# The mLSTM gates' running maximum: products by TensorE, or copies through DRAM by GpSimd

## The chip, the cores and the metric

The kernel is one program on one core of a Trainium2 chip. The metric is the time of one execution on the device, in microseconds (us), as the median of several runs; all inputs lie in the chip's memory beforehand. The difference treated here is a few microseconds of about two milliseconds.

## The reference

A trunk of four residual layers works on 256 tokens of width 2048: an even layer (sliding-window attention beside an mLSTM, one joint input projection), a SwiGLU layer, an odd layer (forgetting attention), another SwiGLU layer. Everything is float32. The change touches the mLSTM of the even layer alone: four heads, keys of width 128, values of width 256, two chunks of 128 tokens. What it computes of the gates:

```python
i_pre = softcap(i_m + b_i)                  # 256 x 4
f_pre = softcap(f_m + b_f)
log_f = jax.nn.log_sigmoid(f_pre)           # in chunks of 128
b = jnp.cumsum(log_f, axis=-1)
...
log_D = b[..., :, None] - b[..., None, :] + log_i[..., None, :]
log_D = jnp.where(causal, log_D, -jnp.inf)
g = b + m_prev[..., None]
m_t = jnp.maximum(g, jnp.max(log_D, axis=-1))
D = jnp.exp(log_D - m_t[..., None])
inter = jnp.exp(g - m_t)
qk = jnp.einsum('bhctd,bhcsd->bhcts', qc, kc) * D
```

The stabiliser m_t is a running maximum along the tokens, one for each head. It is needed in two layouts: along the free dimension, the same on all 128 partitions (for D, whose rows are keys and whose columns are queries), and with tokens on the partitions (for `inter` and the weights of the keys).

## The kernel before

**Matmuls.** Each float32 weight is split into a high and a low part in the reduced format fp32r, and each activation likewise, so that one product is three matmuls (high by high, low by high, high by low). Weights come from DRAM in chunks of 2 x 128 rows by 512 columns (512 KB) through the SyncE queue (L119); ScalarE casts the high part (L173, or L318 for derived operands), VectorE subtracts to get the low part (L174, L319), and TensorE multiplies: 512 columns a matmul. `gemm` walks the 16 tiles of k in eight steps of two. `pair_group` computes two projections at once with seven products in place of eight, over eight positions in an order written out by hand (`MIXQ`, `MIXV`); it derives sums and differences of the weight chunks on VectorE (tiles `hr`) and keeps its sums in PSUM banks of the pools `pa` and `pm`, four banks each.

**Side jobs.** Work that isn't a large matmul is put in between. A list `later` holds pairs of step and function, and `run_due` calls those that are due when a gemm gets to that step; `pair_group` has such a list of its own (`todo`). `Q_STEPS`, `OM_STEPS` and `VM_STEPS` say at which step of which projection each job comes:

- G0 to G4: the mLSTM's gates (below)
- S0 to S2: sums of activations for the seven-product form
- R0 to R3: the second halves of the four groups of sliding-window attention (products of the turned weights `tt` with the values `vs` into `po`, L449, split into `mh` and `ml`)
- J0: the end of one group's transposition by DMA

The projection of `OFF_OM` (o gate, 256 columns), then `OFF_VM` (values), then `pair_even` over the mLSTM's queries and keys (`OFF_QM`, `OFF_KM`) is the stretch from about 126 to 170 us of the profile. Inside it also run the last groups' soft-max (den, rec, `s` times `rec`, L391 and L395) and its transposes (L435, L439).

**Order.** The program is written with tile pools under a scheduler that plans with a timeline of its own and fixes the order of the instructions of each engine; semaphores hold the engines to the dependences. On each engine the order is strict: an instruction that waits holds up all behind it.

**The gates.** `gates_0` caps them and makes -log_sigmoid (`nlf`). `gates_1` makes, in PSUM, the input gate plus the sum of forget gates, with heads on four partitions (`ut`), then by two scans on VectorE the running maximum `mt` (4 x 256), with the chunk's last value in `edge` (4 x 2). `gates_2` fills a PSUM tile `pn` by ten small products: the sums of forget gates with tokens on partitions (`upper` by `nlf`, L880), `mt` turned (by the identity, K = 4, L881), and `edge` on all partitions (by the identity). VectorE copies it to `nat` and makes `un` and `ex`, and ScalarE takes the exponential of `ex`. `gates_3`, twice, for two heads each: four products in all of a selector `sel` (4 x 128, built by GpSimd) with `mt` put the rows of the maximum on all partitions (tile `pb`, L902), VectorE adds the mask `future` into `dt_` (L905), and ScalarE takes four exponentials with `un` as bias (L913). `dt_` is used after the query and key projection, `ex` in the scaling of queries and keys.

The odd layer uses another way for a quantity of the same kind: its summed forget gates are written to DRAM (`scratch`, L1119) and broadcast back to all partitions by GpSimd's queue (L1124), and GpSimd masks them (L1129).

Of the kernel before, what the change touches and what calls it, by code (L numbers as in the profile page):

```python
# [7 lines left out]
F32 = mybir.dt.float32  # L8
# [4 lines left out]
ALU = mybir.AluOpType  # L13
# [4 lines left out]
P = 128  # L18
D = 2048
S = 256  # L20
NT = S // P
KT = D // P
FF = 5632
NB = 512
CK = 2
EPS = 1e-5
NEG = -1.0e30
# [28 lines left out]
Q_STEPS = dict(S0=2, S1=4, R1=6, S2=6, G0=7)  # L56
OM_STEPS = dict(G1=1, J0=3, G2=4, R0=6, G3=7)
VM_STEPS = dict(R2=1, G4=1, R3=4)
PARTS = (0, 3, 7, 11)
# [9 lines left out]
def trunk(  # L69
# [651 lines left out]
    with tc.tile_pool(name="ev", bufs=1) as ev:  # L721
        with tc.issue_after(loaded[0].ins):
# [17 lines left out]
        )  # L740
        future = ev.tile([P, P], F32, name="future")
        nc.gpsimd.memset(future, 0.0)
        nc.gpsimd.affine_select(
            out=future, in_=future, pattern=[[1, P]], compare_op=ALU.is_ge, fill=-NEG, base=0, channel_multiplier=-1
        )

        nk = KVH * HD
# [99 lines left out]
        edge = ev.tile([4, 2], F32, name="edge")  # L847
        nat = ev.tile([P, 3, NT, 4], F32, name="nat")
        un = ev.tile([P, NT, 4], F32, name="un")
        ex = ev.tile([P, 4, 4], F32, name="ex")  # L850
        sel = ev.tile([4, ML_H, P], F32, name="sel")
        dt_ = None
# [7 lines left out]
        def gates_1():  # L860
            pu = pm.tile([P, NB], F32, tag="pm", name="pu")
            for c in range(NT):
# [11 lines left out]
                out=mt[:, P : 2 * P], data0=ut[:, P : 2 * P], data1=ut[:, P : 2 * P], initial=edge[:, 1:2], op0=ALU.max, op1=ALU.max  # L874
            )

        def gates_2():
            pn = pm.tile([P, NB], F32, tag="pm", name="pn")
            for c in range(NT):
                nc.tensor.matmul(pn[:, 4 * c : 4 * c + 4], upper, nlf[:, c, :], start=True, stop=True)  # L880
                nc.tensor.matmul(pn[:, 8 + 4 * c : 12 + 4 * c], mt[:, c * P : (c + 1) * P], ident[0:4, 0:4], start=True, stop=True)  # L881
                nc.tensor.matmul(
                    pn[:, 16 + 4 * c : 20 + 4 * c], edge[:, c : c + 1].broadcast_to([4, P]), ident[0:4, 0:4], start=True, stop=True
                )
            nc.vector.tensor_copy(nat.rearrange("p a c h -> p (a c h)"), pn[:, 0:24])
            nc.vector.tensor_tensor(out=un, in0=ig, in1=nat[:, 0, :, :], op=ALU.add)
            nc.vector.tensor_tensor(out=ex[:, 0:2, :], in0=nat[:, 0, :, :], in1=nat[:, 1, :, :], op=ALU.subtract)
            nc.vector.tensor_tensor(out=ex[:, 2, :], in0=nat[:, 2, 1, :], in1=nat[:, 1, 1, :], op=ALU.subtract)
            nc.vector.tensor_tensor(out=ex[:, 3, :], in0=un[:, 0, :], in1=nat[:, 2, 0, :], op=ALU.subtract)
            nc.scalar.activation(ex, ex, AF.Exp)  # L890

        def gates_3(g):
            nonlocal dt_
            if g == 0:
                dt_ = ev.tile([P, ML_H, NT, P], F32, tag="dt", name="dt_")
                nc.gpsimd.memset(sel, 1.0)
                nc.gpsimd.affine_select(
                    out=sel, in_=sel, pattern=[[-1, ML_H], [0, P]], compare_op=ALU.is_equal, fill=0.0, base=0, channel_multiplier=1
                )
            pb = pm.tile([P, 2, NT, P], F32, tag="pm", name="pb")  # L900
            for i in range(2):
                nc.tensor.matmul(  # L902
                    pb[:, i, :, :].rearrange("p c q -> p (c q)"), sel[:, 2 * g + i, :], mt, start=True, stop=True
                )
            nc.vector.tensor_tensor(  # L905
                out=dt_[:, 2 * g : 2 * g + 2, :, :].rearrange("p h c q -> p (h c) q"),
                in0=pb.rearrange("p h c q -> p (h c) q"),
                in1=future[:, None, :].broadcast_to([P, 4, P]),
                op=ALU.add,
            )  # L910
            for hh in (2 * g, 2 * g + 1):
                for c in range(NT):
                    nc.scalar.activation(  # L913
                        dt_[:, hh, c, :], dt_[:, hh, c, :], AF.Exp, bias=un[:, c, hh : hh + 1], scale=-1.0
                    )
# [7 lines left out]

        jobs = dict(G0=gates_0, G1=gates_1, G2=gates_2, G3=lambda: gates_3(0), G4=lambda: gates_3(1))
        jobs.update((f"S{j}", lambda j=j: sums_q(j)) for j in range(len(mixed_of(MIXQ))))
# [31 lines left out]
        with tc.tile_pool(name="mp", bufs=1) as mp:  # L957
# [9 lines left out]

            def pair_even(c0, c1, order):
                plain, c = pair_group(mp, 0, x_of, sums_m, [(wi, c0), (wi, c1)], order, halves=halves, raws=raws, inner=lambda: None)
# [347 lines left out]
```

## Time and profile before

| | |
|---|---|
| median of 3 runs | 2084.02 us (2083.39 to 2084.61) |
| profiled execution, its own time | 2085.2 us |
| span of the profile | 2083.5 us |
| TensorE (PE) busy | 2073.6 us, 100% |
| VectorE (DVE) busy | 1826.7 us, 88% |
| ScalarE (ACT) busy | 1362.8 us, 65% |
| GpSimd (POOL) busy | 37.8 us, 2% |
| mean granted TensorE clock | 0.998 of full speed |
| DMA | 208 GB/s on average |

The profile is one execution, recorded by the hardware's profiler. Busy time is the union of the recorded instructions of an engine; a matmul's record overlaps with that of the next, so that the distance of their starts, not the length, is what one costs in a row. PEld is the loading of weights, beside PE. The granted clock is that at which TensorE was allowed to run, as a share of full speed. The chain of waits is followed back from the last instruction to whatever released it. Rows in order of time have the start, the length, the engine, the line of the program (L...), the operation, output and inputs, the shape, and how many of them follow one another; brackets hold a wait and what ended it. Rows by windows give, for each stretch of time, the sum and then the busy time and count of PE, PEld, DVE, ACT and POOL, then the granted clock, the share of time in which the DMA engines are busy, and what they move in GB/s.

### The profile page before, as it was taken

To read this page: it belongs to the slowest core of one execution; us is meant where nothing else is said; L and a number is where in the kernel's file an instruction comes from. 1 tells how busy PE (TensorE), PEld (TensorE's weight loads), DVE (VectorE), ACT (ScalarE), POOL (GpSimd) and SP (SyncE) were. 2 spreads that over 40 slices of the span, in tenths; PEclk is the share of its full clock that TensorE was granted. 3 is DMA by queue.
4 is the path that set the end of the run, shared out by engine and by line. 5 is a ranking of instruction groups with operands and counts; after the bars stand their busy time and mean duration, and the time that the engine had idled before them with its cause. 6 is when DMAs were issued, how large, how long until landed. Compare 5 with 4: busy or idle time off the path is not lost.

```text
span 2083.5 us, 27000 instructions
## 1 busy us (share of the span) xinstructions
PE 2073.6 (100%) x9513; PEld 1721.3 (83%) x9513; DVE 1826.7 (88%) x2416; ACT 1362.8 (65%) x1720; POOL 37.8 (2%) x62
## 2 busy tenths in 40 slices
PE   9999999999999999999999999999999999999998
PEld 7878888888888888888888888888888888888887
DVE  6778859999999999999898778679999999999994
ACT  6765568665576656667677777587655667456753
POOL 1000000000000000000000000000000000000000
PEclk9999999999999999999999999999999999999999
DMA  8664668666666666666666866586656667666664
GB/s 293 174 198 149 216 175 253 219 207 206 197 227 218 208 217 209 216 203 212 190 202 211 240 185 191 157 277 220 215 196 208 205 204 238 202 205 208 222 197 139
DMA packets 302616, 432.77 MB, mean 208 GB/s; under 512 B 99584, under 2 KB 107792, under 8 KB 302352
## 3 DMA queue, kind: packets, MB, share of 16 engines
q1 hardware_dynamic: 300432, 424.70, 64.3%
q0 software_dynamic: 1328, 5.26, 0.7%
q8 instruction: 75, 1.23, 0.2%
q10 hardware_dynamic: 720, 1.09, 0.2%
q14 instruction: 61, 0.50, 0.1%
HBM read 408.15 MB, written 2.11 MB: 197 GB/s over the span
## 4 chain that ended last, share of the span: by engine, by line
PE 97%; DVE 1%; ACT 1%; issue 0%; DMA 0%; SPq 0%; POOLq 0%; POOL 0%; ACTq 0%; DVEq 0%
PE acc L488 21%; PE acc L489 21%; PE acc L490 21%; PE acc L209 6%; PE acc L208 5%; PE acc L210 5%; PE prod L488 5%; PE prod L489 5%; PE prod L490 5%; PE p L348 1%; PE po L449 1%; ACT s L382 0%; PE ptm L338 0%; PE po L450 0%; DMA raw<-in_w_in_even_dram 0%
## 5 line engine op out<-in xcount | busy, mean ns | idle before, releaser
L173 ACT CAST hi<-raw 128x1024 fp32r<-128x1024 f32 (+3 forms) x656 | 665.3, 1028 | 445.5 <-PE acc L490 280.1
L174 DVE TENSOR_TENSOR lo<-raw,hi 128x1024 fp32r<-128x1024 f32 (+3 forms) x656 | 772.6, 1192 | 147.0 <-ACT hi L173 144.5
L489 PE MATMUL acc<-lo,xh 128*128 128x512 f32 x1254 | 489.7, 391 | 0.0
L488 PE MATMUL acc<-hi,xh 128*128 128x512 f32 x1254 | 486.3, 390 | 0.0
L490 PE MATMUL acc<-hi,xl 128*128 128x512 f32 x1254 | 485.6, 390 | 0.0
L490 PEld LDWEIGHTS acc<-hi,xl 128*128 128x128 f32 x1254 | 235.8, 188 | 49.1 <-issue 0.3
L488 PEld LDWEIGHTS acc<-hi,xh 128*128 128x128 f32 x1254 | 235.5, 188 | 49.1 <-ACT hi L173 0.2
L489 PEld LDWEIGHTS acc<-lo,xh 128*128 128x128 f32 x1254 | 235.9, 188 | 48.7 <-DVE lo L174 0.2
L489 PE MATMUL acc<-lo,mh 128*128 128x512 f32 x437 | 169.7, 389 | 0.0
L490 PE MATMUL acc<-hi,ml 128*128 128x512 f32 x437 | 168.2, 389 | 0.0
L488 PE MATMUL acc<-hi,mh 128*128 128x512 f32 x437 | 167.9, 389 | 0.0
L318 ACT CAST hi<-raw 128x512 fp32r<-128x512 f32 x109 | 67.7, 621 | 90.4 <-PE acc L490 82.7
L209 PE MATMUL acc<-lo,mh 128*128 128x512 f32 (+1 forms) x322 | 126.2, 392 | 0.0
L208 PE MATMUL acc<-hi,mh 128*128 128x512 f32 (+1 forms) x322 | 125.6, 391 | 0.1
L318 ACT CAST ht<-t 128x1024 fp32r<-128x1024 f32 x95 | 99.9, 1052 | 35.4 <-PE prod L490 33.0
L210 PE MATMUL acc<-hi,ml 128*128 128x512 f32 (+1 forms) x322 | 122.4, 390 | 0.0
L319 DVE TENSOR_TENSOR lt<-t,ht 128x1024 fp32r<-128x1024 f32 x95 | 115.7, 1218 | 4.2 <-ACT ht L318 4.2
L318 ACT CAST ht<-raw 128x1024 fp32r<-128x1024 f32 x95 | 99.7, 1049 | 28.5 <-PE acc L490 13.4
L319 DVE TENSOR_TENSOR lt<-raw,ht 128x1024 fp32r<-128x1024 f32 x95 | 115.7, 1218 | 1.4 <-ACT ht L318 1.3
L209 PE MATMUL acc<-lo,xh 128*128 128x512 f32 (+3 forms) x288 | 99.5, 347 | 0.2 <-DVE lo L174 0.2
L210 PE MATMUL acc<-hi,xl 128*128 128x512 f32 (+3 forms) x288 | 98.1, 344 | 0.0
L208 PE MATMUL acc<-hi,xh 128*128 128x512 f32 (+3 forms) x288 | 95.9, 347 | 0.3 <-ACT hi L173 0.2
(362 smaller groups left out, 3444.4 us busy)
## 6 DMA issues: line engine op xcount, KB each, us to landing
raw<-in_w_gate_dram SPq DMA_DIRECT2D x176, 512.0 KB, 4.4
raw<-in_w_up_dram SPq DMA_DIRECT2D x176, 512.0 KB, 4.6
raw<-in_w_down_dram SPq DMA_DIRECT2D x176, 512.0 KB, 5.1
raw<-in_w_in_odd_dram SPq DMA_DIRECT2D x88, 512.0 KB, 5.1
raw<-in_w_in_even_dram SPq DMA_DIRECT2D x51, 512.0 KB, 4.8
raw<-in_w_out_even_dram SPq DMA_DIRECT2D x32, 512.0 KB, 4.7
raw<-in_w_out_odd_dram SPq DMA_DIRECT2D x32, 512.0 KB, 4.6
hr<-in_w_in_even_dram SPq DMA_DIRECT2D x12, 512.0 KB, 4.6
```

The lines of the kernel that those rows point to most:

```text
L173: latest[0] = nc.scalar.copy(hi[:, k, 0:n], raw[:, k, 0:n])
L174: nc.vector.tensor_tensor(out=lo[:, k, 0:n], in0=raw[:, k, 0:n], in1=hi[:, k, 0:n].bitcast(F32), op=ALU.subtract)
L208: nc.tensor.matmul(o, ah[:, ts], hi, start=(k == 0), stop=False)
L209: nc.tensor.matmul(o, ah[:, ts], lo, start=False, stop=False)
L210: nc.tensor.matmul(o, al[:, ts], hi, start=False, stop=(k == k_all - 1 and cs.stop == n))
L318: nc.scalar.copy(dst_h, src)
L319: nc.vector.tensor_tensor(out=dst_l, in0=src, in1=dst_h.bitcast(F32), op=ALU.subtract)
L348: nc.tensor.matmul(pq[j % 2][:, j // 2, :], q_of(j, b), k_of(j)[:, 0:cols], start=True, stop=True)
L449: nc.tensor.matmul(po, v_of(j, 0), tt[:, j, 0:2, :].rearrange("p c q -> p (c q)"), start=True, stop=False)
L488: nc.tensor.matmul(o, ah, hi, start=start, stop=False)
L489: nc.tensor.matmul(o, ah, lo, start=False, stop=False)
L490: nc.tensor.matmul(o, al, hi, start=False, stop=stop)
```

## The change

The transposed maximum, its copies on all partitions and the edges no longer go over TensorE. `gates_1` also makes the two sums of forget gates (`upper` by `nlf`) into its own PSUM tile, copies them to `nat`, and writes `mt` and `edge` to two DRAM tiles, `rows` and `ends`, through GpSimd's queue. A new job GB (`gates_b`, step 4 of the o projection) reads them back through the same queue: `rows` on all partitions into `dt_` (512 KB), `ends` on all partitions into `edge_b`, and the two halves of `rows` turned into `nat` (one word for each token and head); two selects on GpSimd mask `dt_` (in place of the tile `future` and two additions on VectorE). `gates_2` keeps the small subtractions and one exponential and goes to step 5. The eight exponentials of `gates_3` go together into the query and key projection, at its position 4. R0 and R3 keep their steps; G3 and G4 are gone.

```diff
 Q_STEPS = dict(S0=2, S1=4, R1=6, S2=6, G0=7)
-OM_STEPS = dict(G1=1, J0=3, G2=4, R0=6, G3=7)
-VM_STEPS = dict(R2=1, G4=1, R3=4)
+OM_STEPS = dict(G1=1, J0=3, GB=4, G2=5, R0=6)
+VM_STEPS = dict(R2=1, R3=4)
+G3_AT = 4
...
-        future = ev.tile([P, P], F32, name="future")
-        nc.gpsimd.memset(future, 0.0)
-        nc.gpsimd.affine_select(
-            out=future, in_=future, pattern=[[1, P]], compare_op=ALU.is_ge, fill=-NEG, base=0, channel_multiplier=-1
-        )
...
-        nat = ev.tile([P, 3, NT, 4], F32, name="nat")
+        nat = ev.tile([P, 2, NT, 4], F32, name="nat")
...
-        sel = ev.tile([4, ML_H, P], F32, name="sel")
+        rows = dp.tile([ML_H, S], F32, name="rows")
+        ends = dp.tile([ML_H, 2], F32, name="ends")
+        edge_b = ev.tile([P, ML_H, 2], F32, name="edge_b")
...
         def gates_1():
...
+            for c in range(NT):
+                nc.tensor.matmul(pu[:, 2 * P + 4 + 4 * c : 2 * P + 8 + 4 * c], upper, nlf[:, c, :], start=True, stop=True)
+            nc.gpsimd.dma_start(rows, mt)
+            nc.gpsimd.dma_start(ends, edge)
+            nc.vector.tensor_copy(nat[:, 0, :, :].rearrange("p c h -> p (c h)"), pu[:, 2 * P + 4 : 2 * P + 12])
+
+        def gates_b():
+            nonlocal dt_
+            dt_ = ev.tile([P, ML_H, NT, P], F32, tag="dt", name="dt_")
+            nc.gpsimd.dma_start(dt_.rearrange("p h c q -> p h (c q)"), rows.partition_broadcast(P))
+            nc.gpsimd.dma_start(edge_b, ends.partition_broadcast(P))
+            for c in range(NT):
+                nc.gpsimd.dma_start(nat[:, 1, c, :], rows[:, c * P : (c + 1) * P].rearrange("h p -> p h"))
+            for g in range(0, ML_H, 2):
+                o = dt_[:, g : g + 2, :, :].rearrange("p h c q -> p (h c) q")
+                nc.gpsimd.affine_select(
+                    out=o, in_=o, pattern=[[0, 4], [1, P]], compare_op=ALU.is_ge, fill=-NEG, base=0, channel_multiplier=-1
+                )
 
         def gates_2():
-            pn = pm.tile([P, NB], F32, tag="pm", name="pn")
-            for c in range(NT):
-                nc.tensor.matmul(pn[:, 4 * c : 4 * c + 4], upper, nlf[:, c, :], start=True, stop=True)
-                nc.tensor.matmul(pn[:, 8 + 4 * c : 12 + 4 * c], mt[:, c * P : (c + 1) * P], ident[0:4, 0:4], start=True, stop=True)
-                nc.tensor.matmul(
-                    pn[:, 16 + 4 * c : 20 + 4 * c], edge[:, c : c + 1].broadcast_to([4, P]), ident[0:4, 0:4], start=True, stop=True
-                )
-            nc.vector.tensor_copy(nat.rearrange("p a c h -> p (a c h)"), pn[:, 0:24])
...
-            nc.vector.tensor_tensor(out=ex[:, 2, :], in0=nat[:, 2, 1, :], in1=nat[:, 1, 1, :], op=ALU.subtract)
-            nc.vector.tensor_tensor(out=ex[:, 3, :], in0=un[:, 0, :], in1=nat[:, 2, 0, :], op=ALU.subtract)
+            nc.vector.tensor_tensor(out=ex[:, 2, :], in0=edge_b[:, :, 1], in1=nat[:, 1, 1, :], op=ALU.subtract)
+            nc.vector.tensor_tensor(out=ex[:, 3, :], in0=un[:, 0, :], in1=edge_b[:, :, 0], op=ALU.subtract)
             nc.scalar.activation(ex, ex, AF.Exp)
 
-        def gates_3(g):
...
-            pb = pm.tile([P, 2, NT, P], F32, tag="pm", name="pb")
-            for i in range(2):
-                nc.tensor.matmul(
-                    pb[:, i, :, :].rearrange("p c q -> p (c q)"), sel[:, 2 * g + i, :], mt, start=True, stop=True
-                )
-            nc.vector.tensor_tensor(
-                out=dt_[:, 2 * g : 2 * g + 2, :, :].rearrange("p h c q -> p (h c) q"),
-                in0=pb.rearrange("p h c q -> p (h c) q"),
-                in1=future[:, None, :].broadcast_to([P, 4, P]),
-                op=ALU.add,
-            )
-            for hh in (2 * g, 2 * g + 1):
+        def gates_3():
+            for hh in range(ML_H):
                 for c in range(NT):
                     nc.scalar.activation(
                         dt_[:, hh, c, :], dt_[:, hh, c, :], AF.Exp, bias=un[:, c, hh : hh + 1], scale=-1.0
...
-            c = pair_even(OFF_QM, OFF_KM, MIXQ)
+            c = pair_even(OFF_QM, OFF_KM, MIXQ, [(G3_AT, gates_3)])
```

More of the change, by code (lines that the diff above doesn't have):

```diff
@@ L890, in gates_2 @@
             nc.scalar.activation(ex, ex, AF.Exp)
-        def gates_3(g):
[L893 to L898, printed above, removed]
-                )
-            pb = pm.tile([P, 2, NT, P], F32, tag="pm", name="pb")
-            for i in range(2):
-                nc.tensor.matmul(
-                    pb[:, i, :, :].rearrange("p c q -> p (c q)"), sel[:, 2 * g + i, :], mt, start=True, stop=True
-                )
-            nc.vector.tensor_tensor(
-                out=dt_[:, 2 * g : 2 * g + 2, :, :].rearrange("p h c q -> p (h c) q"),
-                in0=pb.rearrange("p h c q -> p (h c) q"),
-                in1=future[:, None, :].broadcast_to([P, 4, P]),
-                op=ALU.add,
-            )
-            for hh in (2 * g, 2 * g + 1):
+        def gates_3():
+            for hh in range(ML_H):
@@ L922, in sums_q @@
             sums_of(sw, sx[0][:, j, :, :], sx[1][:, j, :, :], whole(xh, xl, pair), tags=("qt", "qt"), bufs=2)
-        jobs = dict(G0=gates_0, G1=gates_1, G2=gates_2, G3=lambda: gates_3(0), G4=lambda: gates_3(1))
+        jobs = dict(G0=gates_0, G1=gates_1, G2=gates_2, GB=gates_b)
         jobs.update((f"S{j}", lambda j=j: sums_q(j)) for j in range(len(mixed_of(MIXQ))))
@@ L966, in trunk, with pair_even @@
             halves = spare_halves()
-            def pair_even(c0, c1, order):
-                plain, c = pair_group(mp, 0, x_of, sums_m, [(wi, c0), (wi, c1)], order, halves=halves, raws=raws, inner=lambda: None)
+            def pair_even(c0, c1, order, todo=()):
+                plain, c = pair_group(mp, 0, x_of, sums_m, [(wi, c0), (wi, c1)], order, todo, halves=halves, raws=raws, inner=lambda: None)
                 for m in range(2):
```

## The prediction

> **What bounds the kernel now.** I read the page first (span, busy shares, chain), then the busy time by windows around the changed steps, then the order in time of TensorE, VectorE, ScalarE and GpSimd there, and last the transfers issued by GpSimd elsewhere in the kernel, since the change adds six of them.
>
> ```profile
> span 2083.5 us, 27000 instructions
> PE 2073.6 (100%) x9513; PEld 1721.3 (83%) x9513; DVE 1826.7 (88%) x2416; ACT 1362.8 (65%) x1720; POOL 37.8 (2%) x62
> PE 97%; DVE 1%; ACT 1%; issue 0%; DMA 0%; SPq 0%; POOLq 0%; POOL 0%; ACTq 0%; DVEq 0%
> ```
>
> TensorE is busy for the whole span and is 97% of the chain that ended last. A microsecond of its queue that goes away is a microsecond of the kernel, unless a wait comes into its place. All the changed steps run between 126 and 170 us; the order of the instructions of the two kernels, compared engine by engine, differs only there. So the question is what TensorE does in these 45 us. The windows (PE, PEld, DVE, ACT, POOL busy, granted clock, DMA share, GB/s):
>
> ```profile
> 135.68:139.10 3.42, 3.42 (x23) 2.75 (x22) 2.57 (x8) 2.68 (x11) 0.00 (x0) 1.00 0.00 0
> 139.10:142.51 3.41, 3.41 (x11) 2.68 (x9) 3.15 (x14) 1.81 (x3) 0.00 (x0) 0.50 0.00 0
> 142.51:145.92 3.41, 3.41 (x17) 2.29 (x16) 2.69 (x4) 2.66 (x8) 0.00 (x0) 1.00 0.00 0
> ```
>
> Two things are to be seen: the granted clock is half from 139.10 to 142.51, and no transfer runs from 135.7 to 145.9. TensorE in order of time (start, length):
>
> ```profile
> 127.67 0.39 PE L880 MATMUL pn<-nlf,upper 128*128 128x4 f32 x2
> 127.98 0.66 PE L449 MATMUL po<-tt,vs 128*64 128x256 f32 x4
> 129.48 0.50 PE L210 MATMUL acc<-hi,xl 128*128 128x512 f32 x1
> 134.83 0.39 PE L489 MATMUL acc<-lo,xh 128*128 128x512 f32 x1
> 135.06 0.39 PE L490 MATMUL acc<-hi,xl 128*128 128x512 f32 x1
> 135.38 0.38 PE L881 MATMUL pn<-ident,mt 4*128 4x4 f32 x2
> 138.24 1.19 PE L435 MATMUL pp<-ident,s 128*128 128x128 f32 x8
> 139.09 0.78 PE L489 MATMUL acc<-lo,xh 128*128 128x512 f32 x1
> 142.59 0.60 PE L439 MATMUL pp<-ident,s 128*128 128x128 f32 x4
> 142.94 0.48 PE L488 MATMUL acc<-hi,xh 128*128 128x512 f32 x1
> 145.55 1.13 PE L902 MATMUL pb<-mt,sel 4*128 4x256 f32 x4
> 146.60 0.50 PE L490 MATMUL acc<-hi,xl 128*128 128x512 f32 x1
> 169.40 0.39 PE L488 MATMUL acc<-hi,hs 128*128 128x512 f32 x1
> ```
>
> **What TensorE gets rid of.** Large matmuls follow each other at 0.23 us (134.83 to 135.06). From 135.29 (135.06 + 0.23) to 138.24 stand all small products on mt and edge and the first pair of pb, 2.95 us. In between are one large matmul (0.23) and one of the two sums of forget gates (0.31, as 127.67 to 127.98), which stay: 2.41 goes. The second pair of pb takes 145.55 to 146.60: 1.05 goes. The two sums stay, as a pair of their own among large matmuls; a change between kinds of product costs some 0.1 (eight transposes up to the next large matmul, 138.24 to 139.09, are 0.85; four, 142.59 to 142.94, are 0.35). Sum: 2.41 + 1.05 - 0.1 = 3.4 us less.
>
> The clock is the second term. From 139.09 to 142.59 eight large matmuls take 3.50 us; at 0.23 and one change they would take 1.94: 1.6 us are lost to the half clock. It follows a window (135.68:139.10) in which the queue held almost nothing but products with four rows, single-column products and transposes. In the changed kernel that stretch is filled with large matmuls: eighteen stand there in a row. I take the 1.6 as won. The Trainium skill ("TensorE: Matmul & The Clock Gate", What's actually happening) says that the clock is set from activity in a free-running window of about 3.4 us, and that a window without enough of it halves the clock; the trace agrees with the length, 139.10 to 142.51 at 0.50.
>
> Against this stand two more changes between kinds: the new order spreads the transposes and the products with vs over eleven blocks, where nine were. That is 0.3 us.
>
> **What takes the place: transfers.** VectorE now waits for them, and it works strictly in order. Its rows, and those of the same pair of operations (write to DRAM, broadcast back) in the odd layer:
>
> ```profile
> 133.70 0.14 DVE L872 TENSOR_TENSOR edge<-mt,ut 4x1 f32<-4x1 f32 x1
> 133.88 0.47 DVE L873 TENSOR_TENSOR_SCAN mt<-ut,edge 4x128 f32<-4x128 f32 x1
> 134.34 1.20 DVE L174 TENSOR_TENSOR lo<-hr,hi 128x1024 fp32r<-128x1024 f32 x1
> 136.30 0.69 DVE L548 TENSOR_TENSOR hr<-hr 128x512 f32<-128x512 f32 x1
> 137.91 0.20 DVE L391 RECIPROCAL rec<-den 128x8 f32<-128x8 f32 x1
> 138.83 1.92 DVE L395 TENSOR_SCALAR s<-s,rec 128x128 f32<-128x128 f32 x8
> 143.23 0.69 DVE L440 COPY tt<-pp 128x512 f32<-128x512 f32 x1 [0.98 <-PE pp L439]
> 143.84 1.22 DVE L174 TENSOR_TENSOR lo<-raw,hi 128x1024 fp32r<-128x1024 f32 x1
> 1052.51 0.56 POOL L1119 DMA_DIRECT2D scratch<-negct  x1 [26.61 <-DMA raw<-in_w_in_odd_dram]
> 1057.33 0.56 POOL L1124 DMA_DIRECT2D cb<-scratch  x1 [4.26 <-DMA scratch<-negct]
> 1064.18 1.20 POOL L1129 TENSOR_SCALAR_AFFINE_SELECT cb<-cb 128x512 f32<-128x512 f32 x1 [6.28 <-DMA cb<-scratch]
> 1259.80 0.55 POOL L1124 DMA_DIRECT2D cb<-scratch  x1 [2.27 <-issue]
> 1264.54 2.17 POOL L1129 TENSOR_SCALAR_AFFINE_SELECT cb<-cb 128x512 f32<-128x512 f32 x1 [4.20 <-DMA cb<-scratch]
> 1054.00:1055.00 1.00, 1.00 (x6) 0.83 (x5) 1.00 (x3) 0.00 (x0) 0.00 (x0) 1.00 0.92 283
> out_dram<-h SPq DMA_DIRECT2D x4, 256.0 KB, 2.6
> DMA to landing us min/median/max: 7.7/9.3/11.2
> ```
>
> *First wait: edge_b.* In the new order VectorE does the lo of hr (134.34 to 135.55), the copies of nat (0.1) and tt (0.6 of new queue time), the two hr differences (0.6 each) and un, and at about 137.7 stands before ex minus edge_b. Behind that instruction are queued den, rec, the lo of hr's second half and the eight products of s with rec; for the first of those products TensorE waits with its transposes. The edge is ready at 133.84, ends is issued at 134.0, edge_b when ends has landed. One such transfer took 4.8 us (1052.51 to 1057.33), with the engines 0.92 taken; the 256 KB stores at the empty end of the kernel took 2.6. Here the engines are at 0.00, so I take 2.6 twice: edge_b at 139.2; ends of the range 139.2 and 143.6. From there to the first product are den 0.2, rec 0.2, lo 0.7 and 0.2: 140.5 (to 144.9).
>
> When does TensorE want it? From 127.67, in the new order: eight po (127.98 to 129.48: 1.5), eight transposes 0.85 (138.24 to 139.09), four more 0.35, the two sums 0.6, eight po again 1.5, thirty-nine large matmuls at 0.23 (9.0) and some nine changes of kind (0.9): 142.4. So the first wait is hidden with 2 us to spare; at the slow end it costs 2.5.
>
> *Second wait: nat.* rows is issued at 134.5 and landed at 137.1. GpSimd then has edge_b, dt_ and the two turned copies to issue, 0.55 each; the second nat starts at about 138.5. For its landing there is no like row: each partition gathers four single words. The nearest in form is the load of h by GpSimd (two runs per partition, the row 7.7/9.3/11.2, but 512 KB in a row of four); the nearest in place is the broadcast on quiet engines, 1259.80 to 1264.54, 4.7. I take 4.7, since the bytes are few: 143.2, range 141.1 (2.6) to 149.7 (11.2). VectorE gets there itself at 139.2 + 0.4 + 0.7 + 1.9 + 0.7 = 142.9, then does the small subtractions (0.3) and a lo (1.22) that TensorE needs for its next matmuls: ready at 144.8 or so. TensorE wants it twelve transposes (1.2), eight large matmuls (1.8) and a few changes (0.5) after 142.4: 145.9. Hidden by 1.1; I allow 0.6 for small waits of this kind (hr's last difference, two ml and the next tt copy, for which TensorE waits too, are queued behind the lo). At the slow end the lo is ready at 151.3, and TensorE stands for 5.4.
>
> **What else moves.** The two adds of future (0.69 each) leave VectorE and become two selects of at most 1.2 each on GpSimd, idle there otherwise; dt_ lands at 137.2 + 4.7, at latest + 6.9 (1057.33 to 1064.18), so it is masked by 147. The eight exponentials move on ScalarE behind the cast of the next hr:
>
> ```profile
> 142.60 1.28 ACT L913 ACTIVATE dt__1317<-dt__1317,un 128x128 f32<-128x128 f32 x4
> 155.05 1.05 ACT L173 CAST hi<-hr 128x1024 fp32r<-128x1024 f32 x1 [3.91 <-PE acc L490]
> 156.00 0.61 ACT L318 CAST hi<-hr 128x512 fp32r<-128x512 f32 x1
> 131.30 14.15 SPq L119 DMA_DIRECT2D raw<-in_w_in_even_dram  x2
> 169.60 2.01 ACT L173 CAST hi<-raw 128x1024 fp32r<-128x1024 f32 x2 [0.99 <-PE acc L490]
> ```
>
> They delay the half-size cast of hr (156.00) by 2.6, and with a mh cast and the ve copies that go ahead of it by 4.4; its product on TensorE is at 169.40, 12.8 later. If that cover went they would cost up to 4.4. The SyncE queue keeps its order; the weight load that waits for the late lo (issued at 145.1, the second of the row at 131.30) is cast at 169.60, so a few us late do no harm. GpSimd's ve memset and its h loads come after and are not needed before 158. These count as nothing.
>
> **The sum.** -3.4 (products) -1.6 (clock) +0.3 (changes of kind) = -4.7, and with +0.6 (small waits) -4.1. The profiled execution took 2085.2 us (span 2083.5), 1.2 above the median of the runs, 2084.0. The work is the same in both, so the sum is put to the median: 2079.9; a profiled execution that lies as high as this one would show 2081.1.
>
> **Rivals.**
>
> *The turned copies are slow (slower).* The second nat lands late, VectorE holds the lo behind it, and TensorE stands; with a stop of more than some 3 us the clock halves again and the 1.6 comes back. For it: 512 single words per copy, no such transfer in the trace, and the h row with 7.7 to 11.2. Against it: engines at 0.00 and 2 KB in each. Break-even is where stop and clock eat the 4.7 won: a stop of 3.1, nat at 147.4. With h's 11.2 the time is 2084.0 - 4.7 + 5.4 + 1.6 = 2086.3; with the two copies one behind the other at h's 7.7 (137.9 + 15.4 = 153.3, lo at 154.9, stop 9.0) it is 2089.9. Chance 0.28. The Trainium skill ("DMA: Bandwidth & Descriptors", Rules for kernel authors) speaks for this rival: a strided last dimension becomes one descriptor per element, and a rearranged copy is not the way to turn data. No run here shows it yet.
>
> *The edge takes the slow price.* Both hops at 4.8: stop of 2.5 at the first transposes, clock lost again (1.6): 2084.0 - 4.7 + 2.5 + 1.6 = 2083.4, no change that counts. The 0.92 row is for it, the 0.00 windows against. Chance 0.14.
>
> *The gate keeps its half clock.* The stretch with transposes and po still leaves one window too thin: only the products are won, 2084.0 - 3.4 + 0.3 + 0.6 = 2081.5. Chance 0.12.
>
> **How the numbers follow.** Forecast case (both waits hidden, 2078.4 to 2081.5): 0.46. About 0.2% or 4.2 us is what a measurement of this kernel can tell from no change, so the bounds are 2079.8 and 2088.2, and the forecast lies beside the first. Of the 0.46, 0.28 falls below 2079.8 and 0.18 above; of the slow copies 0.06 to no change and 0.22 to slower; the edge 0.12 to no change and 0.02 to slower; the gate 0.02 to faster, 0.09 to no change, 0.01 to slower. Faster 0.30, same 0.45, slower 0.25. The range begins at 2078.4: the sum without the small waits (0.6), without the 0.3, and with 0.6 for the changes of kind that go with the removed groups. It ends at 2088.5, which takes in all rivals but the tail of the first.
>
> **What would show it.** Right: no products with four rows left in the windows 135 to 146, clock 1.00 throughout, VectorE waiting for edge_b for 1 to 2 us at about 138 and nat for under 1 us, and the hi of hr on TensorE (169.40 before) at about 165.4. Wrong: a wait of TensorE at the transposes after 142 or at the lo after 145, put down to DMA on VectorE; a clock of 0.50 between 142 and 153; or the two nat copies landing more than 8 us after their issue.

## The result, and the profile after

| | before | after |
|---|---|---|
| median of 13 runs each, side by side | 2084.95 us (2083.39 to 2086.65) | 2080.39 us (2080.02 to 2080.94) |
| ratio | | 0.9979, 95% interval 0.9971 to 0.9986 |
| profiled execution, its span | 2085.2, 2083.5 | 2080.05, 2078.3 |

The change makes the kernel 4.6 us faster by the medians, 5.2 by the two profiled spans. The prediction said 2079.9, 4.1 less than the median it started from. The page of the kernel after, the lines that answer to those of before:

```profile
span 2078.3 us, 26990 instructions
PE 2068.3 (100%) x9497; PEld 1718.1 (83%) x9497; DVE 1826.0 (88%) x2414; ACT 1362.5 (66%) x1720; POOL 41.6 (2%) x66
PE 96%; DVE 2%; issue 1%; ACT 1%; DMA 1%; SPq 0%; POOLq 0%; POOL 0%; ACTq 0%; DVEq 0%
```

TensorE is busy for 2068.3 us where it was for 2073.6; the 5.3 less are the whole gain of this execution. The windows of the kernel after, the same three as before (PE, PEld, DVE, ACT, POOL busy, granted clock, DMA share, GB/s):

```profile
135.68:139.10 3.42, 3.42 (x16) 2.84 (x16) 2.00 (x5) 2.64 (x11) 2.26 (x4) 1.00 0.16 30
139.10:142.51 3.41, 3.41 (x24) 2.36 (x23) 2.63 (x10) 1.64 (x2) 1.37 (x3) 1.00 0.44 132
142.51:145.92 3.41, 3.41 (x23) 2.95 (x22) 3.41 (x9) 1.64 (x3) 0.29 (x1) 1.00 0.00 0
```

The clock stays at 1.00, transfers run in the first two windows, and GpSimd works in all three. In order of time, rows of the kernel after on VectorE, GpSimd and TensorE:

```profile
136.98 0.69 DVE L549 TENSOR_TENSOR hr<-hr 128x512 f32<-128x512 f32 x1
139.84 0.16 DVE L896 TENSOR_TENSOR ex<-un,edge_b 128x4 f32<-128x4 f32 x1 [2.17 <-DMA edge_b<-ends]
140.80 2.68 DVE L396 TENSOR_SCALAR s<-s,rec 128x128 f32<-128x128 f32 x8
143.99 0.16 DVE L894 TENSOR_TENSOR ex<-nat 128x8 f32<-128x8 f32 x1
144.15 1.21 DVE L175 TENSOR_TENSOR lo<-raw,hi 128x1024 fp32r<-128x1024 f32 x1
137.95 1.53 POOL L885 DMA_DIRECT2D nat<-rows  x2
141.53 1.28 POOL L888 TENSOR_SCALAR_AFFINE_SELECT dt__1241<-dt__1241 128x512 f32<-128x512 f32 x2 [2.04 <-DMA dt__1241<-rows]
142.41 0.27 PE L436 MATMUL pp<-ident,s 128*128 128x128 f32 x1
164.18 0.39 PE L489 MATMUL acc<-hi,hs 128*128 128x512 f32 x1
```

The tile `nat` of the kernel after, from issue to landing of its two copies:

```profile
DMA to landing us min/median/max: 3.1/3.4/3.7
```

VectorE stands 2.17 us before the subtraction that reads `edge_b`, and not at all before the one that reads `nat`: the copies land at about 142 (3.1 to 3.7 after issues at 137.9 and 138.7), and VectorE gets there at 143.99. TensorE's first transpose behind the products with `rec` is at 142.41 and waits for nothing. The product of the half-size `hi` of `hr`, at 169.40 before, is at 164.18: the 5.2 are all there by then.

The stretch taken apart, from the first product of `pu` to the first `ptm` behind the query and key projection; every distance between the starts of two rows of TensorE is put to the kind of the first. "Over 0.2275" is what the 215 large matmuls took above 0.2275 us each (changes of kind, stops, half clock):

| us | before | after | difference |
|---|---|---|---|
| first `pu` to first `ptm` | 126.67 to 191.39: 64.72 | 126.71 to 186.17: 59.46 | -5.26 |
| `pn` and `pb` | 1.71 + 2.09 | 0 | -3.80 |
| `pu` (after: with the two sums) | 1.00 | 1.36 | +0.36 |
| `po`, transposes | 5.55 + 2.32 | 5.56 + 2.18 | -0.13 |
| large matmuls over 0.2275 | 3.14 | 1.45 | -1.69 |

The rows are rounded to 0.01, so a sum here can be off by 0.02. The products into `pn` were called ten above; the program has six, and the trace records each as two.

**The clock term is not in every execution.** Beside the experiments there are 97 executions of the kernel before: 40 with a mean granted clock of 0.999, median 2083.6 us, and 57 with 0.998 or less, median 2085.3. In every trace here the clock is half for the last 3 to 6 us as well, when the matmuls are over; that alone gives 0.999, and one half window more gives 0.998. The 1.7 between the medians is what the half window of the profile costs (3.41 us at half clock), and that execution belongs to the second group. But the two groups overlap in time (2082.5 to 2085.8, and 2084.4 to 2088.0), and no trace of an execution of the first group was kept: that this window is what they lack is inferred. All 24 executions of the kernel after (13 here, 11 below) have 0.999 and lie between 2079.57 and 2081.06. So the change is worth some 3.3 us in an execution that would have kept its clock and some 4.9 in one that would not.

### The profile page after: what moved, and what is told of

It reads as the page before. It is cut to its first block, busy times and chain, and to the rows that moved or that the text cites. A ratio compares the mean times of both kernels' runs of the same rounds, so it can differ in the third digit from the quotient of the medians.

```text
span 2078.3 us, 26990 instructions
## 1 busy us (share of the span) xinstructions
PE 2068.3 (100%) x9497; PEld 1718.1 (83%) x9497; DVE 1826.0 (88%) x2414; ACT 1362.5 (66%) x1720; POOL 41.6 (2%) x66
## 4 chain that ended last, share of the span: by engine, by line
PE 96%; DVE 2%; issue 1%; ACT 1%; DMA 1%; SPq 0%; POOLq 0%; POOL 0%; ACTq 0%; DVEq 0%
PE acc L490 21%; PE acc L489 21%; PE acc L491 21%; PE acc L210 6%; PE acc L209 6%; PE acc L211 5%; PE prod L490 5%; PE prod L491 5%; PE prod L489 5%; PE p L349 1%; PE po L450 1%; DVE lo L175 0%; ACT s L383 0%; DMA raw<-in_w_in_even_dram 0%; PE ptm L339 0%
```

## The experiments

Each kernel ran beside the kernel before on the same chip (medians of before there: 2084.88 to 2085.13). Two theories stood against each other: that the gain is two terms, products and clock, with all copies hidden; and that the copies cost and something else pays. A second question came with the clock: what makes a stretch "thin".

**Parts of the change.** `bcast_only`, the kernel after with

```diff
+                nc.tensor.matmul(pn[:, 4 * c : 4 * c + 4], mt[:, c * P : (c + 1) * P], ident[0:4, 0:4], start=True, stop=True)
+                nc.tensor.matmul(pn[:, 8 + 4 * c : 12 + 4 * c], edge[:, c : c + 1].broadcast_to([4, P]), ident[0:4, 0:4], ...)
-                nc.gpsimd.dma_start(nat[:, 1, c, :], rows[:, c * P : (c + 1) * P].rearrange("h p -> p h"))
```

> Of the change only the broadcast of the rows of the maximum, the mask by GpSimd, the sums in step one and the later exponentials; the turned maximum and the edges stay eight small products in gates_2. Theory (products and clock are two separate terms): the eight pb products, 2.09 us of TensorE's queue in the profile of before, are gone, the turned and edge products (some 1.3 us) stay; the stretch of small products is shorter than the 3.4 us of a clock window, so the clock stays at 1.00 and the 1.6 us is won too: about 3.7 us under before. Rival (the turned and edge products beside the transposes are what halves the clock): only 2.1 us under before, with a window at 0.50 near 139 to 143.

`turn_only`, the kernel after with `gates_3(g)`, `sel`, `pb` and `future` as in the kernel before:

```diff
-            nc.gpsimd.dma_start(dt_.rearrange("p h c q -> p h (c q)"), rows.partition_broadcast(P))
...
-                nc.gpsimd.affine_select(out=o, in_=o, pattern=[[0, 4], [1, P]], ...)
...
+                nc.tensor.matmul(pb[:, i, :, :] ..., sel[:, 2 * g + i, :], mt, start=True, stop=True)
+            nc.vector.tensor_tensor(out=dt_[:, 2 * g : 2 * g + 2, :, :] ..., in0=pb ..., in1=future[:, None, :] ..., op=ALU.add)
```

> Of the change only the turned copies and the edges through DRAM and the sums in step one; the rows of the maximum are still put on all partitions by the eight pb products, the mask is added by VectorE and the exponentials stay at their old steps. Theory: the turned and edge products go (1.3 us), pb's 2.1 us stay, and since pb and the twelve transposes behind it make only 2.3 us in a row, the clock stays at 1.00: some 3.0 us under before. Rival (pb and transposes are enough to halve the clock): 1.3 us under before, and a window at 0.50. Rival on the copies: if they were what costs, VectorE would wait for nat for over 1 us.

Measured: `bcast_only` 2083.03 (ratio 0.9992, 0.9983 to 1.0001), `turn_only` 2082.73 (0.9991, 0.9983 to 1.0000), all 22 executions at clock 0.999. Each part alone keeps the clock, so half of the four-row products are not enough to lose it. That is not for a shorter stretch: in `bcast_only` no large matmul stands from 135.09 to 139.48, 4.4 us, and in the kernel before it is 3.8 with one large matmul in it. But neither wins what its products should give: 1.9 and 2.2 where 3.7 and 3.0 were expected. In the same accounting, `bcast_only` has no `pb` (-2.09) but its `po` and transposes take 1.31 more than before: the four pairs that stay are put among the products of `po`, and each charges its neighbours (rows of `bcast_only`; two products on `mt` take 0.31, the two of `po` behind them 0.48, the time of four such where they stand in a row):

```profile
135.09 0.38 PE L889 MATMUL pn<-ident,mt 4*128 4x4 f32 x2
135.40 0.65 PE L450 MATMUL po<-tt,vs 128*64 128x256 f32 x2
135.88 0.38 PE L451 MATMUL po<-tt,vs 128*64 128x128 f32 x2
136.19 0.38 PE L890 MATMUL pn<-ident,edge 4*128 4x4 f32 x2
136.50 0.65 PE L450 MATMUL po<-tt,vs 128*64 128x256 f32 x2
139.48 0.48 PE L490 MATMUL acc<-lo,xh 128*128 128x512 f32 x1
157.53 0.50 PE L489 MATMUL acc<-hi,xh 128*128 128x512 f32 x1 [0.49 <-ACT ve L935]
```

The last row is a stop of TensorE for a copy of `ve` behind the eight exponentials on ScalarE. `turn_only` has stops of 0.20 behind an addition of the mask and 0.49 behind an `ml` on VectorE. So the scheduler's order for a half change is the worse one here; no run holds the order fixed to show it apart.

**What halves the clock.** `full_rows`, the kernel before with

```diff
-        mt = ev.tile([4, S], F32, name="mt")
+        mt = ev.tile([P, S], F32, name="mt")
+        nc.gpsimd.memset(mt, 0.0)
...
-                nc.tensor.matmul(pn[:, 8 + 4 * c : 12 + 4 * c], mt[:, c * P : (c + 1) * P], ident[0:4, 0:4], ...)
+                nc.tensor.matmul(pn[:, 8 + 4 * c : 12 + 4 * c], mt[:, c * P : (c + 1) * P], ident[:, 0:4], ...)
```

and `edge` and `sel` likewise:

> The kernel before with the same products in the same order, but mt, edge and the selector are 128 partitions high, filled up with zeros, so that every small product uses all 128 rows of the array. If the clock falls because four-row products leave the array's rows unused, it stays at 1.00 here and the time is 1.6 us under before. If it falls because a whole window of 3.4 us holds nothing but short products, whatever their height, the window at 0.50 stays at 139 to 143 and the time is that of before within 0.5 us.

`spread_steps`, the kernel before with other steps:

```diff
-OM_STEPS = dict(G1=1, J0=3, G2=4, R0=6, G3=7)
-VM_STEPS = dict(R2=1, G4=1, R3=4)
+OM_STEPS = dict(G1=1, J0=3, G2=3, R0=6)
+VM_STEPS = dict(R2=1, G3=4, R3=4, G4=5)
```

> The kernel before with all its products, only at other steps (G2 at 3 of the o projection, G3 and G4 at 4 and 5 of the value projection), so that large matmuls stand between pn, the first pb and the second pb. If the half clock comes from the small products standing in one stretch, it goes without any DMA: clock 1.00 from 126 to 170 us and 1.6 us under before, plus or minus 0.3 for two or three more changes of kind. If small products as such do it, a window at 0.50 shows up behind one of the groups and the time is that of before or up to 1.6 us more.

`full_long`, `full_rows` with

```diff
-            for i in range(2):
+            for i in (0, 1, 0, 1) if g == 0 else (0, 1):
                 nc.tensor.matmul(pb[:, i, :, :] ..., sel[:, 2 * g + i, :], mt, start=True, stop=True)
```

> The kernel before with its small products 128 rows high (as in the earlier run) and the first pair of pb made twice over, so that the stretch of short products grows from 3.1 to 4.0 us, longer than the 3.8 us in the kernel before. If the length of the stretch halves the clock, at least as large a share of the executions as before (20 of 33) shows a granted clock of 0.998 and lies some 1.7 us above the others. If the height does it, all executions show 0.999 and lie within about 1 us, at 2082.65 + 0.9 = 2083.5.

Measured: `full_rows` 2082.65 (0.9992, 0.9983 to 1.0001), `spread_steps` 2084.39 (0.9999, 0.9990 to 1.0008), `full_long` 2083.41 (0.9993, 0.9984 to 1.0002); all 33 executions at 0.999. `full_long` settles that length is not the cause: its stretch of short products (its rows below) is 3.9 us, where that of the kernel before, 3.8 us, lost its clock in 57 of 97, and it loses none in 11.

```profile
135.50 0.28 PE L883 MATMUL pn<-ident,mt 128*128 128x4 f32 x2
139.36 0.47 PE L489 MATMUL acc<-lo,xh 128*128 128x512 f32 x1
```

It is the four-row products, then; with 128 rows the same products keep the clock. Whether the clock leaves out the rows that stand unused, or the time that TensorE loses at the steps to and from such products (below, some 0.7 us of the stretch), these runs do not tell apart, since the zeros take away both. `spread_steps` keeps the clock with four-row products that no longer stand together, but it is only 0.5 under the median of before, where 1.6 was expected, and 0.8 over the group of before that kept its clock: its order is worse.

`full_rows` shows a second thing. It is 2.2 under the median of before, more than the clock, and 1.0 under the group of before that kept its clock, with the same order on TensorE. Its rows beside those of before (the pair on `mt` 135.38 to 135.69 there, and the two below):

```profile
136.98 0.36 PE L882 MATMUL pn<-ident,edge 4*128 4x4 f32 x2
137.20 1.10 PE L902 MATMUL pb<-mt,sel 4*128 4x256 f32 x4
```

```profile
135.41 0.28 PE L883 MATMUL pn<-ident,mt 128*128 128x4 f32 x2
135.55 0.47 PE L488 MATMUL acc<-hi,xh 128*128 128x512 f32 x1
135.87 0.28 PE L884 MATMUL pn<-ident,edge 128*128 128x4 f32 x2
136.00 0.36 PE L882 MATMUL pn<-nlf,upper 128*128 128x4 f32 x2
136.45 0.36 PE L884 MATMUL pn<-ident,edge 128*128 128x4 f32 x2
136.67 1.11 PE L904 MATMUL pb<-mt,sel 128*128 128x256 f32 x4
137.62 1.04 PE L435 MATMUL pp<-ident,s 128*128 128x128 f32 x8
143.31 1.13 PE L904 MATMUL pb<-mt,sel 128*128 128x256 f32 x4
144.09 0.58 PE L490 MATMUL acc<-hi,xl 128*128 128x512 f32 x1
```

A pair on `mt` takes 0.14 where it took 0.31, the second pair of `pb` 0.78 where it took 1.05. But behind others of their kind four-row products are no slower: the pair on `edge` takes 0.22 in both (136.98 to 137.20, 136.45 to 136.67). So it is not the product that costs but the step between heights, some 0.1 to 0.2 us each. From the first pair on `mt` to the transposes it comes to 0.65 (135.38 to 138.24 before, 135.41 to 137.62 here). The Trainium skill ("TensorEngine Tiling (Array Packing)", Key Properties) says that changing the tiling mode drains TensorE; the rows agree with that, though none shows the drain itself, nor that a product of four rows is such a mode. Zeros in 124 partitions, no transfer at all, bring half of what the change brings.

**Does it matter when the copies land?** `late_turn6`, the kernel after with

```diff
+            for c in range(6):
+                nc.gpsimd.dma_start(spare[:, c, :], rows[:, (c % NT) * P : (c % NT + 1) * P].rearrange("h p -> p h"))
             for c in range(NT):
                 nc.gpsimd.dma_start(nat[:, 1, c, :], rows[:, c * P : (c + 1) * P].rearrange("h p -> p h"))
```

> The changed kernel with six more turned copies of the maximum, into a tile that nobody reads, ahead of the two that are needed; nothing is held, so the scheduler, which plans with the longer queue, puts the subtractions that read nat some six instructions later on VectorE. Each copy is issued in 0.77 us, so nat lands about 4.6 us later, near 147. Theory (a late copy costs only where it meets an instruction that TensorE needs next): VectorE gets to the subtractions at about 149 and does not wait; 2080.4 plus or minus 0.4. Rival (turned copies cost by their many single words, one behind the other): nat lands after 150, VectorE waits, and the time is over 2082.

`late_pin8`, the kernel after with eight broadcasts of `rows` to DRAM in that place, and one `lo` queued on VectorE behind the subtraction that reads `nat`:

```diff
+            for i in range(8):
+                nc.gpsimd.dma_start(heap[:, i, :, :], rows.partition_broadcast(P))
...
-            nc.vector.tensor_tensor(out=lo[:, k, 0:n], ...)
+            with tc.issue_after(held) if held is not None else nullcontext():
+                nc.vector.tensor_tensor(out=lo[:, k, 0:n], ...)
```

> The changed kernel with eight more copies of the rows of 512 KB each, DRAM to DRAM, in GpSimd's queue ahead of the turned copies, and the lo of the next weight chunk held behind the subtractions that read nat, so that the late nat meets the work that TensorE wants. This is the rival of the slow turned copies made true. At 1.4 to 4.0 us a copy nat lands between 153 and 174; TensorE wants the lo at about 151.5 in this order and gets it 1.5 us after nat. Theory: the stop is nat's landing plus 1.5 minus 151.5, so at least 3 us and most likely near 10, and the clock halves once more behind it (1.6): 2084 to 2095. If VectorE's wait did not matter, 2080.4.

`late_pin8` measured 2090.08 (1.0025, 1.0015 to 1.0035), 9.7 over the kernel after. Its tile `nat`, its windows, and its rows in order of time:

```profile
DMA to landing us min/median/max: 17.7/18.9/20.1
```

```profile
160.00:165.00 5.00, 0.03 (x1) 0.00 (x0) 0.00 (x0) 0.00 (x0) 0.00 (x0) 0.74 0.68 176
165.00:170.00 5.00, 3.26 (x8) 2.58 (x9) 4.68 (x7) 2.63 (x4) 0.00 (x0) 0.50 0.43 126
170.00:175.00 5.00, 5.00 (x18) 3.98 (x17) 5.00 (x7) 2.37 (x3) 0.00 (x0) 0.74 0.66 203
```

```profile
165.31 0.17 DVE L900 TENSOR_TENSOR ex<-nat 128x8 f32<-128x8 f32 x1 [12.75 <-DMA nat<-rows]
166.74 0.79 PE L493 MATMUL acc<-lo,xh 128*128 128x512 f32 x1 [6.72 <-DVE lo L178]
172.76 0.40 PE L492 MATMUL acc<-hi,xh 128*128 128x512 f32 x1
```

The mechanism of the rival is as it was drawn: a late `nat`, VectorE standing 12.75 us, the `lo` behind it, TensorE standing 6.72, and then half clock. The clock costs more than the 1.6 of the rival: the fourteen large matmuls from 166.74 to 172.76 take 6.0 us where 3.2 would do, 2.8 lost. And the point at which it decides was put too early: TensorE had work until 160.0, not 151.5, since the scheduler had put other matmuls ahead. This is the order of `late_pin8`; where the order of the kernel after would break even was not measured.

`late_turn6` measured 2082.43 (0.9988, 0.9979 to 0.9997), 2.0 over the kernel after, and not for the reason of either theory: nobody waits for `nat`, which lands at about 145, while VectorE gets to it at 149.91. On VectorE and GpSimd of `late_turn6`:

```profile
140.29 2.58 DVE L396 TENSOR_SCALAR s<-s,rec 128x128 f32<-128x128 f32 x8
142.79 1.11 DVE L550 TENSOR_TENSOR hr<-hr,hr 128x512 f32<-128x512 f32 x1
143.82 1.66 DVE L175 TENSOR_TENSOR lo<-raw,hi 128x1024 fp32r<-128x1024 f32 x1
145.40 1.11 DVE L551 TENSOR_TENSOR hr<-hr,hr 128x512 f32<-128x512 f32 x1
143.50 2.46 POOL L891 TENSOR_SCALAR_AFFINE_SELECT dt__1242<-dt__1242 128x512 f32<-128x512 f32 x2
147.65 0.50 PE L489 MATMUL acc<-mh,xh 128*128 128x512 f32 x1 [0.70 <-ACT mh L319]
```

VectorE's differences of `hr` take 1.11 in place of 0.69 and a `lo` 1.66 in place of 1.22, and GpSimd's selects 2.46 in place of 1.28. The `lo` and the second difference stand beside the selects; the first difference would have been over before they began at 143.50, and stood beside the issue of the last turned copy. The `mh` behind the last `hr` is late, and TensorE stands 0.70. The large matmuls take 1.1 more than in the kernel after in the same accounting; where the rest of the 2.0 is, stays open (in the profiled execution, which is 1.8 longer, 0.7 of it lies behind the stretch of the table).

**The mask and the exponentials.** `mask_dve`, the kernel after with the mask tile added by VectorE:

```diff
-                nc.gpsimd.affine_select(out=o, in_=o, pattern=[[0, 4], [1, P]], compare_op=ALU.is_ge, fill=-NEG, ...)
+                nc.vector.tensor_tensor(out=o, in0=o, in1=future[:, None, :].broadcast_to([P, 4, P]), op=ALU.add)
```

> The changed kernel with the mask put back to VectorE: two additions of a mask tile to dt_ after its broadcast has landed, in place of the two selects by GpSimd. In the profile after, the eight products of s with rec took 2.68 us while GpSimd's selects ran, against 1.92 before. Theory (the selects and VectorE hinder each other; both are covered): the eight products are back at 1.92, VectorE has 1.4 us of additions more, and TensorE, which has cover of about 1 us there, loses 0 to 0.7 us: 2080.4 to 2081.1. Rival (the select was the part that made the change pay): over 1.4 us slower than the changed kernel.

`exp_old`, the kernel after with the exponentials back at their steps, four each:

```diff
-OM_STEPS = dict(G1=1, J0=3, GB=4, G2=5, R0=6)
-VM_STEPS = dict(R2=1, R3=4)
+OM_STEPS = dict(G1=1, J0=3, GB=4, G2=5, R0=6, G3=7)
+VM_STEPS = dict(R2=1, G4=1, R3=4)
```

> The changed kernel with the eight exponentials of dt_ back at their old steps (7 of the o projection, 1 of the value projection) rather than at position 4 of the query and key projection. They then stand on ScalarE ahead of casts and wait for GpSimd's mask, which ends at 142.8. Theory (the place of the exponentials is of no account as long as the cast behind them has cover): within 0.5 us of the changed kernel. Rival (a wait in ScalarE's queue holds up the casts that TensorE and VectorE need next): 1 to 2 us over it, with TensorE waiting behind the transposes.

Measured: `mask_dve` 2080.96 (2079.60 to 2081.62), `exp_old` 2080.70 (2080.17 to 2081.33); the ranges overlap that of the kernel after, so neither part is worth anything that these runs resolve. VectorE in `mask_dve`:

```profile
140.42 1.92 DVE L396 TENSOR_SCALAR s<-s,rec 128x128 f32<-128x128 f32 x8
142.86 1.29 DVE L894 TENSOR_TENSOR dt__1246<-dt__1246,future 128x512 f32<-128x512 f32 x2
```

The eight products are back at 1.92. Moving the mask to GpSimd took 1.29 off VectorE and put 0.76 back on, by the slower products.

**Further in the same direction.** `after_again` is the kernel after, for comparison. `un_turned` drops the two sums too:

```diff
-                nc.tensor.matmul(pu[:, 2 * P + 4 + 4 * c : 2 * P + 8 + 4 * c], upper, nlf[:, c, :], start=True, stop=True)
+            nc.gpsimd.dma_start(urows, ut[:, 0 : 2 * P])
...
+                nc.gpsimd.dma_start(un[:, c, :], urows[:, c * P : (c + 1) * P].rearrange("h p -> p h"))
```

and `sums_first` makes them ahead of the copy of `ut`:

```diff
+            for c in range(NT):
+                nc.tensor.matmul(pu[:, 2 * P + 4 + 4 * c : 2 * P + 8 + 4 * c], upper, nlf[:, c, :], start=True, stop=True)
             nc.vector.tensor_copy(ut, pu[0:4, 0 : 2 * P + 1])
```

> The changed kernel once more, as the measure for the three beside it. Theory (the clock term is won because the window of small products is gone): all its executions lie within some 1 us, 2080.0 to 2081.0, with a granted clock of 0.999, while those of the kernel before fall into two groups, 2083.1 to 2084.1 at 0.999 and 2084.7 to 2086.1 at 0.998.

> One step further than the change: the two sums of forget gates with tokens on partitions (two products, in the profile after 0.36 us of TensorE) are not made at all; un is the turned copy of ut, written to DRAM and read back like the maximum, and the sums are un minus the input gate. Theory (small products cost their time on TensorE, hidden copies cost nothing): 0.4 to 0.5 us under the changed kernel, 2080.0. Rival (GpSimd's queue becomes too long: three more descriptors' issues of 0.5 to 0.8 us put nat behind 144): VectorE waits for nat, up to 1 us over the changed kernel.

> The changed kernel with the two sums of forget gates made right behind the other products of the first gates step, into the same PSUM tile, before ut is copied from it. Nothing is added or left out, but the order becomes more compact: the sums stand in one block with the nine products before them and the last twelve transposes in one block, so that TensorE changes between kinds of product some five times less. Theory (what is left of TensorE's queue above 0.23 us a large matmul are those changes, some 0.07 to 0.1 each): 0.3 to 0.5 us under the changed kernel, 2079.9 to 2080.1. Rival (the twelve transposes in one block wait for the products of s with rec, which stand behind edge_b on VectorE): a stop of up to 2 us at the transposes, slower than the changed kernel.

Measured: `after_again` 2080.35 (ratio 0.9979, 0.9971 to 0.9988), `un_turned` 2080.38, `sums_first` 2081.13. In `un_turned` the 0.36 of the sums is won, but a stop of 0.58 comes; in `sums_first` the changes of kind do go (the large matmuls over 0.2275 fall from 1.45 to 0.88) but a stop of 1.22 comes. The stop of `un_turned`, then that of `sums_first`, in order of time on TensorE:

```profile
149.31 0.32 PE L451 MATMUL po<-tt,vs 128*64 128x128 f32 x1 [0.58 <-DVE tt L441]
```

```profile
151.45 0.72 PE L489 MATMUL prod<-mh,hs 128*128 128x512 f32 x2 [1.22 <-ACT mh L319]
```

No version beat the kernel after.

## Why the prediction was right, point by point

- **Products, -3.4.** Shown: -3.80 for `pn` and `pb`, +0.36 for the two sums, -3.44. What the working did not see is that part of it is the step between heights (`full_rows`), where the products themselves cost what others of their size do.
- **Clock, -1.6.** Shown in size (-1.69 with everything else that large matmuls lose), and its cause: the four-row products that stand together (`full_long`, `spread_steps`), with the open point named there. Wrong as a fixed term. The sentence "The work is the same in both, so the sum is put to the median" failed: the profiled execution is one of those that lost their clock, the first three runs (median 2084.0) were by their times a mix, and the other runs moved that median to 2084.95. The same term is 0 or 1.7, so the change gives 3.3 or 4.9.
- **Changes of kind, +0.3, and small waits, +0.6.** Neither is there: the kinds change 26 times before and 24 times after, `po` and transposes take 0.13 less, and no stop of TensorE stands in the stretch. The blocks of `po` and transposes (ten before by the trace, not nine; eleven after) had been counted without those of `pn` and `pb` that go.
- **The size, in part luck.** Products and clock alone are -5.0, what an execution that loses its clock gains. The 0.9 that was added for changes of kind and small waits is not there, but it made up for counting the clock in full: 4.1 forecast, 4.6 by the medians. The `hi` of `hr`, forecast at about 165.4, was at 164.18.
- **First wait.** Forecast: VectorE there at 137.7, the edge at 139.2, the products with rec from 140.5, TensorE's transposes at 142.4. Measured: 137.67 (136.98 + 0.69), 139.8 after a wait of 2.17, 140.80, 142.41.
- **Second wait.** Forecast `nat` at 143.2, VectorE there at 142.9. Measured: at about 142 and 143.99; VectorE came later by the 0.6 of the edge and because its eight products took 2.68, not 1.92, beside the selects. The step that counted GpSimd's selects as nothing was wrong; the cover was forecast at 1.1, and no stop came.
- **Exponentials, nothing.** Borne out by `exp_old` within 0.4.
- **The rivals.** The slow copies did not come: 3.1 to 3.7 us a copy. Made true (`late_pin8`), they cost what the rival said in kind, with more for the clock and a later point at which TensorE runs dry. The edge was 0.6 later than taken, not 4.4. The clock did not keep its half.

## What to carry to other kernels

Before costing a clock episode seen in one profile, look at the granted clock of every execution: a term that is there in half of them moves a median by anything between nothing and its full size. Products with few rows cost more here than their own time, at each step to full height and by the clock they lose; filling the operands up with zeros is the cheapest test of that, and half a cure. A transfer that replaces a product is free as long as nothing that TensorE needs next is held up behind the instruction that reads it; ask also what the engine that issues it does to the others meanwhile.

## What the runs showed of the hardware

- The half clock comes in some executions and not in others of the same program: 57 of 97, by the mean clock. The Trainium skill ("TensorE: Matmul & The Clock Gate", What's actually happening) says that the window runs free of the kernel's start; the two groups fit that. That four-row products bring it about and the same products with 128 rows do not is shown by `full_rows` and `full_long` alone.
- GpSimd and VectorE hinder each other in both directions: a select beside VectorE's two-operand instructions took 1.23 in place of 0.64 each, the VectorE instructions 0.4 longer. The Trainium skill ("SBUF — State Buffer", SBUF: two separate sides) describes a port pair that the two share under an exclusive lock; the rows agree. In `late_turn6` the eight products were slowed, 2.58, with no select running, while GpSimd issued turned copies (138.28 to 143.50); almost all of the delay is in the last two of the eight, though the copies were being issued beside the others too, so its cause stays open:

```profile
138.28 3.73 POOL L886 DMA_DIRECT2D spare<-rows  x5
142.00 1.50 POOL L888 DMA_DIRECT2D nat<-rows  x2
```

- The turned copies were not slow, and do not show as one packet a word: in the trace of the kernel after the two are 32 packets of 128 bytes. The page of before, then that of after:

```profile
DMA packets 302616, 432.77 MB, mean 208 GB/s; under 512 B 99584, under 2 KB 107792, under 8 KB 302352
```

```profile
DMA packets 302919, 433.29 MB, mean 208 GB/s; under 512 B 99756, under 2 KB 107968, under 8 KB 302656
```

Packets under 512 bytes rose by 172, with 1024 single words in the two copies. The rule that the prediction weighed (one descriptor for each element) cost nothing that shows here; only the issue on GpSimd is longer, 0.77 us against 0.54.
